# A two-layer diffusion backbone on one core: layer 0's queries and keys in pairs of token tiles, one modulation vector more on VectorE, idle matmuls and paired squares at the start, and layer 1's scores cut 256 + 384

## The chip, the core and the metric

The kernel runs on one core of a Trainium2 chip. The core has TensorE (PE; its weight loads are listed apart as PEld), VectorE (DVE), ScalarE (ACT), GpSimd (POOL) and SyncE (SP), which issues nearly all transfers. The metric is the device time of one execution in microseconds; lower is better.

## The reference

All numbers are float32. 512 latent tokens and 256 context tokens of width 1024 pass two layers; the output is the latent stream.

```python
for i in range(2):
    mod = silu(c) @ ada_w[i] + ada_b[i]          # six vectors of 1024: shift, scale, gate, twice
    u = rms_norm(h, g_mix[i]) * (1 + sc1) + sh1  # latent and context tokens, each with their own c
    if i == 0:   # 2-D neighbourhood attention, 16 heads of 64, relative position bias
        q, k, v = split(u @ na_wqkv); q, k = rms_norm(q, q_gain), rms_norm(k, k_gain)   # per head
        y = softmax(q k^T / 8 + bias over neighbours, and all context keys) v
    else:        # sliding window of 128, 4 key heads, sink logits, rotary
        y = softmax(q k^T / 8 over keys within 128 of the query, all context keys, a sink) v
    h = h + ga1 * (y @ wo)
    h = h + ga2 * (relu((rms_norm(h, g_mlp[i]) * (1 + sc2) + sh2) @ w1) ** 2 @ w2)
```

## The kernel before

**Products.** A float32 product is made of three matmuls of 32-bit "r" operands (fp32r): high times high, high times low, low times high. So each value that enters a matmul is first split by ACT (the high part, a CAST) and DVE or POOL (the rest, a TENSOR_TENSOR). Tokens stand in six tiles of 128: 0 to 3 latent, 4 and 5 context; the model width is eight blocks of 128, called f as features and k as a contraction.

**Start.** `load` (L701) chains the first loads in a fixed order on SP: the latent tokens (`xT`, four loads of two blocks), then, by `LOADS` (L560), eight pairs of loads of `ada01` (the weights of the first two modulation vectors), four loads of `wqkv00` ("w") and the context tokens ("c"). `stats` (L1423) squares each block of the latent tokens and sums over the width with a float32 matmul by `ones` into bank pq4; ACT then takes Ln and Exp (`st.finish`). `ada01(f)` (L1396) multiplies silu(c) by one block's weights, 16 narrow matmuls into pq0 or pq1; `mods01(f)` (L1409) copies that on ACT, turns it with a matmul by `pair`, and DVE makes shift and 1 + scale of it. `mod0` (L1435) makes u of block f, and the products of k = f for the tiles follow in banks pq2 to pq7.

**Layer 0's queries and keys.** Heads go in eight pairs p. `qkv0(p)` (L1010) multiplies six tiles; per tile, `front(t)` copies 128 queries and 128 keys out of PSUM into a ring `xr` (values go to V), `head_norm` (L964) takes four sums of squares and an inverse root by a chain of eight small operations on ACT and DVE, and `dup_mult` and a second multiply write the scaled rows to a ring `natr`. `back(t, nat)` turns them with three PE transposes and splits the result into the operands T1, T2 (queries) and KK (keys): ACT writes the high part, DVE the rest. `attn0(p)` (L1123) makes scores in banks pq0 and pq1, adds the bias read from DRAM tables (`bias_i`, `bias_e`, written at the start by `bias_tables`, L931, as 32 DRAM-to-DRAM copies), and goes on to the softmax, PE transposes and the product with V.

**Modulation.** The vectors 2 to 5 of layer 0 are made beside the attention: `ada_pe` (L767) on PE for the vectors in `PEK` (four groups of eight 32 x 256 matmuls per vector, into pq5; weights `in_ada_w`, two buffers), `ada_rows` (L745) on DVE for those in `DVK` (eight rows per vector, each one load of 512 KB of `in_ada0` into one buffer and three multiply-and-reduce operations: 1024 wide for latents, twice 512 for the context). `DVN[p]` says how many rows are written into stage p.

**Layer 1's scores.** `Head1.front` (L2021) makes per head and latent tile a row of scores: 512 columns for the outer tiles, and for the inner ones (1 and 2) 640, as 512 in pq0 or pq1 and 128 in pq2; DVE shifts and reduces each part.

**What sets the order.** All calls are recorded as steps, and `Plan.search` (L465) lays them out on the engines with its own list of costs and a seeded random search, stretch by stretch; it may also choose between ACT, DVE and POOL for a step that has two forms. So a change in one place moves instructions in all of the program. Every instruction has L548 or a line near it as its line, since all are issued there; tiles tell them apart.

Of the kernel before, what the change touches and what calls it, by code (L numbers as in the profile page):

```python
# [565 lines left out]
def _build(nc, tc, a, es):  # L566
# [443 lines left out]
    def qkv0(p):  # L1010

        T1, T2, KK = views0(p)[:3]

        def products(ps, t, ks):
            sH, sL = tok((uH_lat, uH_ctx), t), tok((uL_lat, uL_ctx), t)
            for k in ks:
                mm(ps, sH(k), W0[p, k][0], k == 0, False)
                mm(ps, sH(k), W0[p, k][1], False, False)
                mm(ps, sL(k), W0[p, k][0], False, k == KT - 1)

        def front(t):
# [12 lines left out]
            gv.tensor_tensor(out=nat[:, 256:384].rearrange("p (h d) -> p h d", h=2), in0=x[:, 128:256].rearrange("p (h d) -> p h d", h=2), in1=r[:, 2:4].unsqueeze(2).broadcast_to([128, 2, DH]), op=ALU.mult)  # L1034
            return nat

        def back(t, nat):
# [3 lines left out]
            pq = pt[:, 0:256].rearrange("p (h n) -> p h n", h=2)
            pk = pt[:, 256:384]
            if t < 3:
                parts = [(0, 128, 64 + t * 128)]
            elif t == 3:
                parts = [(0, 64, 448), (64, 128, 0)]
            else:
                parts = [(0, 128, t * 128)]
# [13 lines left out]
        nats = {}  # L1062
        if p == 0:
            lat, ctx = range(4), range(4, 6)
            for ts, ks in (*((lat, (k,)) for k in range(LATE + 1)), (ctx, range(LATE + 1)), *((range(6), (k,)) for k in range(LATE + 1, KT - LAST))):
# [4 lines left out]
            load0(1, (0, 1))  # L1070

        order = (0, 3, 4, 5, 1, 2) if p == 0 else range(6)
        for j, t in enumerate(order):
            if p == 0:
                products(banks[2 + t], t, range(KT - LAST, KT))
            nats[t] = front(t)
            if p == 0 and j == 1:
                load0(1, (2, 3))
            if 0 < p < 7 and t == 2:
                load0(p + 1, (0, 1))  # L1080
            if 0 < p < 7 and t == 5:
                load0(p + 1, (2, 3))
# [929 lines left out]
    class Head1:  # L2012
# [8 lines left out]
        def front(self):  # L2021
# [2 lines left out]
            nms, sms, ess = small(4), sums_of(h // 2)[:, h % 2 * 4 : h % 2 * 4 + 4], small(4)  # L2024
            for t in (1, 0, 2, 3):
                q0 = t * 128
                ps = p_sc.next()
                inner = t in (1, 2)
                if t == 0:
                    scores(ps, T1, T2, q0, with_context(K, 0))  # L2030
                    mk = FA[:, 4096:4864].rearrange("p (s n) -> p s n", s=2)[:, :, 0:256]
                    col[t] = {0: 256, 1: 384, 4: 0, 5: 128}
                else:
                    scores(ps, T1, T2, q0, with_context(K, t - 1))
                    mk = in2(mask[:, 0:512])
                    col[t] = {t - 1: 256, t: 384, t + 1: 512, 4: 0, 5: 128}
                n0 = nsink[:, h : h + 1]
                if inner:
                    px = banks[2][:, 128 * (t - 1) : 128 * t]
# [1 line left out]
                    n1 = small()
                    v.tensor_tensor_reduce(out=P[t][:, 512:640], in0=px, in1=mask[:, 512:640], scale=-1.0, scalar=n0, op0=ALU.add, op1=ALU.min, accum_out=n1)
                    n0 = n1
                nm = nms[:, t : t + 1]
                v.tensor_tensor_reduce(out=in2(P[t][:, 0:512]), in0=in2(ps), in1=mk, scale=-1.0, scalar=n0, op0=ALU.add, op1=ALU.min, accum_out=nm)
# [190 lines left out]
```

## Time and profile before

| | us |
|---|---|
| median of 3 runs (lowest, highest) | 1545.16 (1543.29, 1547.68) |
| the profiled execution: its time, its span | 1545.8, 1544.0 |
| busy: PE, PEld | 1520.9, 1349.8 |
| busy: DVE, ACT, POOL | 1237.5, 848.2, 228.3 |

The span is what the profiler saw of that execution; 1.8 us lie around it. Busy time is that in which at least one instruction of the engine ran. [...] PE is busy for 99% of the span, and the chain that ended last is 93% PE.

### The profile page before, as it was taken

Reading aid. Unit: us, or ns where it says so; the run is one execution under the profiler, and the core shown is the slowest. Engines: PE = TensorE matmul, PEld = TensorE weight load, DVE = VectorE, ACT = ScalarE, POOL = GpSimd, SP = SyncE. Lnnn points to the kernel's source line nnn. Section 1 sums busy time; section 2 is a strip of 40 time slices with the busy share of each in tenths; the row PEclk is TensorE's granted clock in tenths of the full one; section 3 lists DMA queues with packets and bytes.
Section 4 is the critical chain, followed back from the end, with each engine's and each line's share of the span. In section 5 each row is a group of like instructions: output and inputs, shape, how many; then the busy total and the mean of one; then the engine's idle time right before and its main releaser. Section 6 shows DMA issues by size and latency. Waiting matters only on the chain.

```text
span 1544.0 us, 26106 instructions
## 1 busy us (share of the span) xinstructions
PE 1520.9 (99%) x9541; PEld 1349.8 (87%) x9541; DVE 1237.5 (80%) x2672; ACT 848.2 (55%) x1989; POOL 228.3 (15%) x223
## 2 busy tenths in 40 slices
PE   7999999999999999999999999999999999999999
PEld 4879888898899999999999998888778989898897
DVE  4888888868579998988888778898876897777764
ACT  4676656677366443334433454577784754455551
POOL 1110000101111222200210001321100312111110
PEclk9999999999999999999999999999999999999999
DMA  9554443215435433345444332011145343323321
GB/s 360 156 179 125 137 164 108 75 38 158 148 104 162 129 120 121 125 144 150 155 133 149 97 100 98 21 34 47 34 155 173 105 128 104 101 84 108 97 69 69
DMA packets 81473, 183.88 MB, mean 119 GB/s; under 512 B 9104, under 2 KB 26048, under 8 KB 81344
## 3 DMA queue, kind: packets, MB, share of 16 engines
q1 hardware_dynamic: 81344, 182.21, 37.3%
q8 instruction: 75, 1.23, 0.3%
q14 instruction: 54, 0.44, 0.1%
HBM read 172.64 MB, written 12.68 MB: 120 GB/s over the span
## 4 chain that ended last, share of the span: by engine, by line
PE 93%; DVE 3%; ACT 2%; DMA 1%; issue 1%; SPq 0%; POOL 0%; DVEq 0%; ACTq 0%; POOLq 0%
PE pq L548 93%; DVE FA L548 1%; DVE RA L548 1%; ACT FA L548 1%; DVE R L548 0%; ACT RA L548 0%; DMA R<-inv_d 0%; DMA FA<-bias_e 0%; ACT R L548 0%; DVE smalls L548 0%; DMA FA<-in_xT_dram 0%; SPq L548 0%; ACT smalls L548 0%; DVE mods L548 0%; POOL FA L548 0%
## 5 line engine op out<-in xcount | busy, mean ns | idle before, releaser
L548 PE MATMUL pq<-RA 128*128 128x256 f32 (+2 forms) x5906 | 1067.9, 334 | 8.1 <-DVE RA L548 4.4
L548 PEld LDWEIGHTS pq<-RA 128*128 128x128 f32 x5906 | 919.0, 189 | 94.7 <-issue 6.2
L548 PE MATMUL pq<-RA,R 128*128 128x256 f32 (+2 forms) x1896 | 339.5, 331 | 1.4 <-DVE FA L548 1.4
L548 ACT CAST RA<-FA 128x512 fp32r<-128x512 f32 (+4 forms) x390 | 232.3, 618 | 170.3 <-PE pq L548 124.3
L548 PEld LDWEIGHTS pq<-RA,R 128*128 128x128 f32 x1896 | 299.1, 189 | 26.5 <-DVE FA L548 2.5
L548 DVE TENSOR_TENSOR RA<-FA,RA 128x512 fp32r<-128x512 f32 (+4 forms) x350 | 256.3, 752 | 35.3 <-ACT RA L548 31.5
L548 DVE SCALAR_TENSOR_TENSOR FA<-pq,mods,FA 128x512 f32<-128x512 f32 (+1 forms) x323 | 197.5, 627 | 98.4 <-PE pq L548 96.0
L548 ACT ACTIVATE FA<-FA 128x256 f32<-128x256 f32 (+2 forms) x216 | 102.8, 483 | 58.6 <-DVE FA L548 47.2
L548 ACT CAST R<-FA 128x512 fp32r<-128x512 f32 x107 | 65.2, 619 | 104.3 <-PE pq L548 94.0
L548 PE MATMUL pq<-ident,FA 128*128 128x128 f32 x772 | 118.4, 274 | 2.0 <-issue 1.4
L548 POOL TENSOR_TENSOR RA<-FA,RA 128x512 fp32r<-128x512 f32 (+3 forms) x40 | 57.8, 1450 | 382.4 <-ACT RA L548 330.8
L548 ACT ACTIVATE FA<-FA,smalls 128x512 f32<-128x512 f32 (+1 forms) x120 | 88.7, 740 | 33.6 <-DVE smalls L548 32.8
L548 PEld LDWEIGHTS pq<-ident,FA 128*128 128x128 f32 x772 | 91.8, 141 | 14.0 <-issue 4.6
L548 DVE TENSOR_TENSOR FA<-FA 128x512 f32<-128x512 f32 (+3 forms) x163 | 88.8, 558 | 7.8 <-ACT FA L548 3.8
L548 ACT COPY R<-pq 128x512 f32<-128x512 f32 (+4 forms) x166 | 74.0, 469 | 34.2 <-PE pq L548 33.2
L548 ACT COPY FA<-pq 128x256 f32<-128x256 f32 (+5 forms) x114 | 44.3, 388 | 85.5 <-PE pq L548 82.8
L548 POOL TENSOR_TENSOR FA<-FA,smalls 128x256 f32<-128x256 f32 (+2 forms) x55 | 37.5, 682 | 294.6 <-DVE smalls L548 232.6
L548 DVE CUSTOM_DVE_ANT_0 R<-R,cst 128x512 bf16<-128x512 f32 (+1 forms) x64 | 79.7, 1245 | 0.4 <-DMA R<-in_ada_dram 0.2
L548 ACT CAST RA<-R 128x256 fp32r<-128x256 f32 (+2 forms) x107 | 51.4, 489 | 51.5 <-PE pq L548 46.8
L548 DVE TENSOR_TENSOR R<-FA,R 128x512 fp32r<-128x512 f32 (+1 forms) x101 | 74.3, 743 | 6.5 <-ACT R L548 5.5
L548 POOL TENSOR_TENSOR FA<-FA 128x256 f32<-128x256 f32 (+2 forms) x50 | 46.0, 927 | 186.3 <-ACT FA L548 85.7
L548 PE MATMUL pq<-R 128*64 128x256 f32 (+3 forms) x432 | 67.2, 450 | 1.1 <-DVE FA L548 1.1
(107 smaller groups left out, 1155.3 us busy)
## 6 DMA issues: line engine op xcount, KB each, us to landing
FA<-in_w_dram SPq DMA_DIRECT2D x128, 256.0 KB
FA<-in_w_dram SPq DMA_DIRECT2D x64, 512.0 KB
R<-in_ada_dram SPq DMA_DIRECT2D x54, 512.0 KB
FA<-in_ada_dram SPq DMA_DIRECT2D x26, 512.0 KB
FA<-in_wqkv_dram SPq DMA_DIRECT2D x24, 384.0 KB
FA<-in_ada_w_dram SPq DMA_DIRECT2D x16, 512.0 KB
FA<-in_wo_dram SPq DMA_DIRECT2D x16, 512.0 KB
FA<-in_wq_dram SPq DMA_DIRECT2D x8, 512.0 KB
```

The costliest lines, as they stand in the source:

```text
L548: tc.keep_in_program_order(getattr(e, f)(*map(real, args), **{k: real(x) for k, x in kw.items()}))
```

## The change

There are five edits.

1. `back`, `front` and the new `scaled` treat two tiles at a time: one `head_norm` of eight sums in place of two of four, and one set of wider splits. `xr` becomes one buffer of 512 in place of two of 256, `natr` two of 768 in place of three of 512. The pairs are (0, 3), (4, 5), (1, 2) for p = 0, else (0, 1), (2, 3), (4, 5).
2. Vector 3 of layer 0 goes from `ada_pe` to `ada_rows`: PE has four groups in place of eight, DVE 24 rows in place of 16. `run(ad)` then stands before stage 2, and from there on `p_mm` has two banks (before, from stage 4).
3. In `stats`, DVE adds the squares of two blocks, and PE has four matmuls by `ones` in place of eight.
4. `busy(10, ones)` issues ten 128 x 128 float32 matmuls of `ones` by `ones` into pq7, which nothing reads, ahead of the statistics.
5. An inner tile of layer 1 has its scores as 256 columns (context) in pq2 and 384 (window) in pq0 or pq1: for 16 heads, two tiles and T1 and T2, 64 matmuls of each width.

```diff
-PEK, DVK, DVN = (2, 3), (4, 5), (0, 4, 3, 3, 3, 3)
+PEK, DVK, DVN = (2,), (3, 4, 5), (0, 5, 5, 5, 5, 4)
-    smalls = pool.tile([128, 24, 4], F32, name="smalls", tag="smalls")
+    smalls = pool.tile([128, 24, 8], F32, name="smalls", tag="smalls")
-    xr = Ring(FA, FX + 1536, 256, 2)
+    xr = Ring(FA, FX + 1536, 512, 1)
-    natr = Ring(FA, FX + 7168, 512, 3)
+    natr = Ring(FA, FX + 7168, 768, 2)
...
-        def front(t):
+        def front(t, x, e):
...
-            x = xr.next()
-            sv.copy(x, ps[:, 0:256])
+            sv.copy(x.rearrange("p (w n) -> p w n", w=2)[:, :, 128 * e : 128 * e + 128], ps[:, 0:256].rearrange("p (w n) -> p w n", w=2))
...
+        def scaled(x):
             nat = natr.next()
-            r = head_norm(x, nat[:, 0:256], 4)
-            dup_mult(nat[:, 0:256], x[:, 0:128], r[:, 0:2], 2)
-            gv.tensor_tensor(out=nat[:, 256:384]..., in0=x[:, 128:256]..., in1=r[:, 2:4]..., op=ALU.mult)
+            r = head_norm(x, nat[:, 0:512], 8)
+            dup_mult(nat[:, 0:512], x[:, 0:256], r[:, 0:4], 4)
+            gv.tensor_tensor(out=nat[:, 512:768]..., in0=x[:, 256:512]..., in1=r[:, 4:8]..., op=ALU.mult)
             return nat
-        def back(t, nat):
-            pt = (p_tr if p else p_ad).next()
-            for i in range(3):
-                pe.transpose(pt[:, i * 128 : i * 128 + 128], nat[:, i * 128 : i * 128 + 128], ident[:])
+        def back(ts, nat):
+            pt, pk = [(p_tr if p else p_ad).next() for _ in range(2)]
+            for e in range(2):
+                for h in range(2):
+                    pe.transpose(pt[:, h * 256 + e * 128 :][:, 0:128], nat[:, (2 * e + h) * 128 :][:, 0:128], ident[:])
+            for e in range(2):
+                pe.transpose(pk[:, e * 128 : e * 128 + 128], nat[:, 512 + e * 128 : 640 + e * 128], ident[:])
...
-        order = (0, 3, 4, 5, 1, 2) if p == 0 else range(6)
-        for j, t in enumerate(order):
...
+        last = None
+        for j, ts in enumerate(((0, 3), (4, 5), (1, 2)) if p == 0 else ((0, 1), (2, 3), (4, 5))):
+            x = xr.next()
+            for e, t in enumerate(ts):
...
+                front(t, x, e)
...
+                if not e:
+                    yield
+                    if last:
+                        back(*last)
+            last = ts, scaled(x)
             yield
...
             q = sq.next()
             squared(q, h(f))
-            pe.matmul(ps[:, 0 : st.n], ones[:], q, start=f == 0, stop=f == KT - 1)
+            if f % 2:
+                v.tensor_tensor(out=q, in0=last, in1=q, op=ALU.add)
+                pe.matmul(ps[:, 0 : st.n], ones[:], q, start=f == 1, stop=f == KT - 1)
+            last = q
...
+    def busy(n, x):
+        for _ in range(n):
+            pe.matmul(banks[7][:, 0:128], ones[:], x[:, 0:128], start=True, stop=True)
+
     more(5)
+    busy(10, ones)
...
-        if p < 4:
-            n = (1, 3, 3, 3)[p]
+        if p < 2:
+            n = (1, 4)[p]
...
-                if inner:
-                    px = banks[2][:, 128 * (t - 1) : 128 * t]
-                    scores(px, T1, T2, q0, K[:, q0 + 384 : q0 + 512])
...
+                if t in (1, 2):
+                    px, ps, n1 = banks[2][:, 256 * (t - 1) : 256 * t], ps[:, 0:384], small()
+                    scores(px, T1, T2, q0, K[:, 0:256])
+                    scores(ps, T1, T2, q0, K[:, q0 + 128 : q0 + 512])
+                    col[t] = {t - 1: 256, t: 384, t + 1: 512, 4: 0, 5: 128}
+                    shifted(P[t][:, 0:256], px, mask[:, 0:256], n0, n1)
+                    shifted(P[t][:, 256:640], ps, mask[:, 256:640], n1, nm)
```

The planner lays everything out anew. Three places follow; R00_132 and R00_134 are the buffer of squares, FA_64 and RA_63 the large working buffers, s32_82 silu(c), pair_93 the small turning matrix, and pq0_66 to pq7_73 the PSUM banks.

PE at the very start, before:

```order
L548 MATMUL pq4_70<-R00_132,ones_76 128x512 x8
L548 MATMUL pq0_66<-FA_64,s32_82 32x128 x16
L548 MATMUL pq1_67<-FA_64,s32_82 32x128 x8
L548 MATMUL pq0_66<-pair_93,FA_64 128x4
L548 MATMUL pq1_67<-FA_64,s32_82 32x128 x8
L548 MATMUL pq0_66<-FA_64,s32_82 32x128 x8
L548 MATMUL pq2_68<-RA_63 128x512 x3
L548 MATMUL pq3_69<-RA_63 128x512 x3
L548 MATMUL pq4_70<-RA_63 128x512 x3
L548 MATMUL pq5_71<-RA_63 128x512 x3
L548 MATMUL pq1_67<-pair_93,FA_64 128x4
L548 MATMUL pq0_66<-R00_132,s32_82 32x128 x8
```

and after:

```order
L548 MATMUL pq7_73<-ones_76 128x128 x10
L548 MATMUL pq4_70<-R00_134,ones_76 128x512 x3
L548 MATMUL pq0_66<-FA_64,s32_82 32x128 x8
L548 MATMUL pq4_70<-R00_134,ones_76 128x512
L548 MATMUL pq0_66<-FA_64,s32_82 32x128 x8
L548 MATMUL pq0_66<-pair_93,FA_64 128x4
L548 MATMUL pq1_67<-FA_64,s32_82 32x128 x8
L548 MATMUL pq3_69<-RA_63 128x512 x2
L548 MATMUL pq1_67<-FA_64,s32_82 32x128 x8
L548 MATMUL pq3_69<-RA_63 128x512
L548 MATMUL pq1_67<-pair_93,FA_64 128x4
L548 MATMUL pq2_68<-RA_63 128x512 x3
```

The idle matmuls are first; `ada01(0)` moved in among the statistics, and `ada01(1)` with its `pair` matmul moved in among the first three products (pq3) of k = 0, where it stood behind all twelve.

ACT at the start, before (squares of the statistics in R00_132, Ln, Exp, the split of `wqkv00`'s first load, the copy of `ada01(0)`, the first high part of u):

```order
L548 ACTIVATE sg_83<-cst_79 128x16
L548 ACTIVATE R00_132<-FA_64 128x512 x4
L548 ACTIVATE FA_64<-pq4_70,eps_77 128x512
L548 ACTIVATE FA_64<-FA_64 128x512
L548 CAST RA_63<-FA_64 128x1024
L548 COPY FA_64<-pq0_66 128x128
L548 ACTIVATE RA_63<-FA_64,mods0_84 128x512
L548 COPY FA_64<-pq1_67 128x128
```

and after:

```order
L548 ACTIVATE R00_134<-FA_64 128x512
L548 ACTIVATE sg_83<-cst_79 128x16
L548 ACTIVATE R00_134<-FA_64 128x512 x3
L548 ACTIVATE FA_64<-pq4_70,eps_77 128x512
L548 COPY FA_64<-pq0_66 128x128
L548 ACTIVATE FA_64<-FA_64 128x512
L548 CAST RA_63<-FA_64 128x1024
L548 ACTIVATE RA_63<-FA_64,mods0_84 128x512
```

The copy of pq0 now stands ahead of Exp and of the split, which it stood behind.

SP from the end of the bias tables to the first reads of them (`in_wqkv02` are weights of p = 2, `in_ada_w` the weights for `ada_pe`, `in_ada0` a row for DVE), before:

```order
L548 DMA bias_i_88<-in_rpb_i_dram 16x8x256
L548 DMA bias_e_89<-in_rpb_dram 16x8x128
L548 DMA FA_64<-in_wqkv02_dram 128x768 x2
L548 DMA FA_64<-in_ada_w_dram 128x1024 x2
L548 DMA FA_64<-in_ada0_dram 128x1024
L548 DMA FA_64<-bias_i_88 128x256 x2
L548 DMA FA_64<-bias_e_89 64x128 x4
L548 DMA FA_64<-in_wqkv02_dram 128x768 x2
```

and after:

```order
L548 DMA bias_i_88<-in_rpb_i_dram 16x8x256
L548 DMA bias_e_89<-in_rpb_dram 16x8x128
L548 DMA FA_64<-in_wqkv02_dram 128x768 x2
L548 DMA FA_64<-in_ada0_dram 128x1024
L548 DMA FA_64<-bias_i_88 128x256
L548 DMA FA_64<-bias_e_89 64x128 x2
L548 DMA FA_64<-bias_i_88 128x256
L548 DMA FA_64<-bias_e_89 64x128 x2
```

The `in_ada_w` loads moved ahead, to places among the earlier table copies, so that three loads of weights stand between the tables' last copy and their first read, where there were five; and the reads for the first head now come before those for the second.

More of the change, by code (lines that the diff above doesn't have):

```diff
@@ L1033, in front @@
-            dup_mult(nat[:, 0:256], x[:, 0:128], r[:, 0:2], 2)
-            gv.tensor_tensor(out=nat[:, 256:384].rearrange("p (h d) -> p h d", h=2), in0=x[:, 128:256].rearrange("p (h d) -> p h d", h=2), in1=r[:, 2:4].unsqueeze(2).broadcast_to([128, 2, DH]), op=ALU.mult)
-            return nat
-        def back(t, nat):
-            pt = (p_tr if p else p_ad).next()
-            for i in range(3):
-                pe.transpose(pt[:, i * 128 : i * 128 + 128], nat[:, i * 128 : i * 128 + 128], ident[:])
[L1041 to L1048, printed above, removed]
+            r = head_norm(x, nat[:, 0:512], 8)
@@ new lines, in scaled, with place @@
+            dup_mult(nat[:, 0:512], x[:, 0:256], r[:, 0:4], 4)
+            gv.tensor_tensor(out=nat[:, 512:768].rearrange("p (h d) -> p h d", h=4), in0=x[:, 256:512].rearrange("p (h d) -> p h d", h=4), in1=r[:, 4:8].unsqueeze(2).broadcast_to([128, 4, DH]), op=ALU.mult)
+            return nat
+        def back(ts, nat):
[5 more added lines that the diff above has]
+                pe.transpose(pk[:, e * 128 : e * 128 + 128], nat[:, 512 + e * 128 : 640 + e * 128], ident[:])
+            pq, pk = pt.rearrange("p (h n) -> p h n", h=2), pk[:, 0:256].rearrange("p (e n) -> p e n", e=2)
+            def place(t):
+                return ([(0, 64, 448), (64, 128, 0)] if t == 3 else [(0, 128, t * 128 + (64 if t < 3 else 0))])
+            parts = []
+            for e, t in enumerate(ts):
+                for lo, hi, at in place(t):
+                    lo, hi = lo + 128 * e, hi + 128 * e
+                    if parts and parts[-1][1] == lo and parts[-1][2] + lo - parts[-1][0] == at:
+                        parts[-1] = (parts[-1][0], hi, parts[-1][2])
+                    else:
+                        parts.append((lo, hi, at))
@@ L1052, in back @@
                 ops.append((T1[:, :, at : at + hi - lo], T2[:, :, at : at + hi - lo], pq[:, :, lo:hi], gq, gq))
-            at = (t + 2) % 6 * 128
+            a0, a1 = ((t + 2) % 6 for t in ts)
             for i in range(2):
-                ops.append((KK[0:64, i, at : at + 128], KK[64:128, i, at : at + 128], pk[64 * i : 64 * i + 64], gk[64 * i : 64 * i + 64], gk[0:64]))
+                K = KK[:, i].rearrange("p (b n) -> p b n", n=128)[:, a0 : a1 + 1 : a1 - a0]
+                ops.append((K[0:64], K[64:128], pk[64 * i : 64 * i + 64], gk[64 * i : 64 * i + 64], gk[0:64]))
             for oH, oL, of, by, by_l in ops:
@@ L1060, in back @@
                 v.scalar_tensor_tensor(out=oL, in0=of, scalar=by_l, in1=oH.bitcast(F32), op0=ALU.mult, op1=ALU.subtract)
-        nats = {}
         if p == 0:
@@ L1070, in qkv0 @@
             load0(1, (0, 1))
-        order = (0, 3, 4, 5, 1, 2) if p == 0 else range(6)
-        for j, t in enumerate(order):
[L1074 to L1082, printed above, removed]
+        last = None
+        for j, ts in enumerate(((0, 3), (4, 5), (1, 2)) if p == 0 else ((0, 1), (2, 3), (4, 5))):
+            x = xr.next()
+            for e, t in enumerate(ts):
+                if p == 0:
+                    products(banks[2 + t], t, range(KT - LAST, KT))
+                front(t, x, e)
+                if p == 0 and 2 * j + e == 1:
+                    load0(1, (2, 3))
+                if 0 < p < 7 and t == 2:
+                    load0(p + 1, (0, 1))
+                if 0 < p < 7 and t == 5:
+                    load0(p + 1, (2, 3))
+                if not e:
[3 more added lines that the diff above has]
+            last = ts, scaled(x)
             yield
-            if j:
-                back(order[j - 1], nats[order[j - 1]])
-        back(order[5], nats[order[5]])
+        back(*last)
         yield
@@ L2026, in front, with shifted @@
                 q0 = t * 128
-                ps = p_sc.next()
-                inner = t in (1, 2)
-                if t == 0:
+                ps, nm, n0 = p_sc.next(), nms[:, t : t + 1], nsink[:, h : h + 1]
+                def shifted(out, ps, mk, n0, nm):
+                    v.tensor_tensor_reduce(out=out, in0=ps, in1=mk, scale=-1.0, scalar=n0, op0=ALU.add, op1=ALU.min, accum_out=nm)
+                if t in (1, 2):
[5 more added lines that the diff above has]
+                    shifted(P[t][:, 256:640], ps, mask[:, 256:640], n1, nm)
+                elif t == 0:
                     scores(ps, T1, T2, q0, with_context(K, 0))
-                    mk = FA[:, 4096:4864].rearrange("p (s n) -> p s n", s=2)[:, :, 0:256]
                     col[t] = {0: 256, 1: 384, 4: 0, 5: 128}
+                    shifted(in2(P[t][:, 0:512]), in2(ps), FA[:, 4096:4864].rearrange("p (s n) -> p s n", s=2)[:, :, 0:256], n0, nm)
                 else:
                     scores(ps, T1, T2, q0, with_context(K, t - 1))
-                    mk = in2(mask[:, 0:512])
                     col[t] = {t - 1: 256, t: 384, t + 1: 512, 4: 0, 5: 128}
-                n0 = nsink[:, h : h + 1]
-                if inner:
-                    px = banks[2][:, 128 * (t - 1) : 128 * t]
-                    scores(px, T1, T2, q0, K[:, q0 + 384 : q0 + 512])
[L2041 to L2045, printed above, removed]
+                    shifted(in2(P[t][:, 0:512]), in2(ps), in2(mask[:, 0:512]), n0, nm)
                 s.activation(P[t], P[t], AF.Exp, bias=nm, scale=-1.0, accum_out=sms[:, t : t + 1])
```

## The prediction

> **What bounds the kernel now.** I read the page first (PE busy 99%, chain 93% PE), then the busy time by stretch, then PE's waits, then the chain from the start on. By stretch (from:to and length in us; busy PE, PEld, DVE, ACT and POOL, with instructions; granted clock, DMA share, GB/s):
>
> ```profile
> 5.58:15.41 9.83, 9.82 (x16) 4.00 (x16) 2.09 (x4) 1.89 (x3) 0.00 (x0) 1.00 1.02 383
> 15.41:20.92 5.51, 3.33 (x83) 2.27 (x82) 2.23 (x5) 3.18 (x6) 0.00 (x0) 1.00 1.06 385
> 20.92:37.88 16.96, 15.75 (x159) 12.05 (x159) 9.39 (x19) 8.48 (x20) 4.39 (x4) 0.90 1.00 396
> 37.88:68.75 30.87, 30.62 (x202) 25.42 (x203) 24.71 (x68) 16.95 (x44) 2.86 (x9) 1.00 0.52 127
> 68.75:82.99 14.24, 11.18 (x90) 8.98 (x89) 12.70 (x41) 11.02 (x36) 1.80 (x3) 1.00 0.85 256
> 80.00:100.00 20.00, 17.81 (x135) 15.70 (x131) 17.41 (x56) 16.27 (x46) 2.45 (x4) 0.91 0.41 127
> 82.99:300.00 217.01, 213.59 (x1445) 188.89 (x1446) 188.58 (x544) 146.75 (x427) 22.55 (x33) 0.99 0.42 134
> ...
> 983.00:1162.00 179.00, 177.54 (x1226) 146.54 (x1226) 152.37 (x462) 132.51 (x327) 30.42 (x39) 1.00 0.20 63
> ```
>
> After 83 us PE hardly waits (3.4 us of 217, 1.5 of 179): there only less work on PE shortens the kernel. The first 83 us are another matter: PE idles 2.2 + 1.2 + 0.3 + 3.1 us, runs the statistics slowly, and waits in a chain. From the chain, in order of time:
>
> ```profile
> 1.19 3.69 DMA FA<-in_xT_dram
> ...
> 5.58 9.91 PE pq L548 x16
> ...
> 16.77 1.04 ACT RA L548
> ...
> 27.83 7.53 PE pq L548 x60
> ...
> 75.84 6.13 DMA FA<-bias_e
> ```
>
> PE is held by the statistics to 15.4, then by ACT (the weights' split at 16.77 ahead of the small copy) to 20.92, and at 82 by the bias table's read. But DMA is saturated to 37.88 (share 1.0): what lands by then can't land sooner, only be used sooner.
>
> **The start, step by step.** Rows of the timeline (start, length, engine, instruction):
>
> ```profile
> 10.02 0.34 PEld L548 LDWEIGHTS pq<-R,ones 128*128 128x128 f32 x1 [0.52 <-issue]
> 10.87 0.34 PEld L548 LDWEIGHTS pq<-R,ones 128*128 128x128 f32 x1 [0.52 <-issue]
> 11.44 0.63 ACT L548 ACTIVATE R<-FA 128x512 f32<-128x512 f32 x1 [1.56 <-DMA FA<-in_xT_dram]
> 12.09 0.69 DVE L548 TENSOR_TENSOR R<-FA 128x512 f32<-128x512 f32 x1 [1.99 <-PE pq L548]
> 12.32 0.19 PEld L548 LDWEIGHTS pq<-R,ones 128*128 128x128 f32 x1 [0.24 <-issue]
> 12.75 0.19 PEld L548 LDWEIGHTS pq<-R,ones 128*128 128x128 f32 x1 [0.24 <-issue]
> 15.52 0.69 ACT L548 ACTIVATE FA<-pq,eps 128x512 f32<-128x512 f32 x1 [3.45 <-PE pq L548]
> 16.24 0.63 ACT L548 ACTIVATE FA<-FA 128x512 f32<-128x512 f32 x1
> 17.71 0.26 ACT L548 COPY FA<-pq 128x128 f32<-128x128 f32 x1
> 20.15 0.72 ACT L548 ACTIVATE RA<-FA,mods 128x512 fp32r<-128x512 f32 x1 [2.18 <-DVE FA L548]
> 25.56 0.28 PE L548 MATMUL pq<-pair,FA 128*128 128x4 f32 x2
> 37.88 12.73 PE L548 MATMUL pq<-RA 128*128 128x512 f32 x54 [0.18 <-ACT RA L548]
> ```
>
> Eight float32 matmuls of 512 are 16 passes; a pass takes 0.86 us at first (10.02 to 10.87) and 0.43 later. Ten idle ones of 128 are 20 passes of a quarter, 20 x 0.215 = 4.3 us from about 1.1 us on, while PE has nothing; their cover is the wait for the first tokens (4.9), and without it they would cost at most those 4.3 less 3.8. Pairing needs one DVE addition (0.69) per two blocks; with the last tokens at 11.44, square 0.65, addition 0.69 and handoffs bring the last pair to about 12.9, and `ada01(0)`'s first half stands ahead. Then two passes: the statistics end at 13.9 to 15.6 (warm to cold) instead of 15.41; I take 14.3, as the passes from 11.4 on were fast even here.
>
> Then Ln 0.69 + copy 0.26 + Exp 0.63 + split 1.04 (beside DVE's product) + high part 0.72 + 0.15 of handoffs = 3.5 us, where it was 5.51, as the chain of `ada01(0)` and the split no longer stand in a row. First product at 17.8 instead of 20.92: 3.1 us less. Next, block 1's `pair` matmul stood behind twelve products of k = 0 (25.56), and k = 1 began at 27.83; now it stands after three. PE's rows up to the context's first products hold 48 products where they held 36. One product takes (12.73 - 0.40) / 53 = 0.233 us, so twelve are 2.8 us. The last of these blocks lands late whatever PE does, so I put the context's start at 35.3 rather than 37.88 (2.6 less). With one `ada01` more left to do behind it (about 0.9) the gain at 68.75 is 2.8 + 2.6 - 0.9 = 4.5 us. Its ends: 0, if the landings hold the block behind, and 7.
>
> **From 68.75 to 82.99** PE idles 3.06 us, and its first `ada_pe` group there takes 2.0 us instead of 1.0:
>
> ```profile
> 78.98 1.12 PE L548 MATMUL pq<-FA,s 128*32 128x256 f32 x16
> 79.46 0.16 PEld L548 LDWEIGHTS pq<-FA,s 128*32 128x32 f32 x8 [0.32 <-DMA FA<-in_ada_w_dram]
> 97.98 1.07 PE L548 MATMUL pq<-FA,s 128*32 128x256 f32 x16
> ```
>
> Its weights now come among the table copies, so sooner. SP's table copies start when the fourth split of weights frees a buffer, so they follow PE's and ACT's lead forward, and three loads instead of five stand ahead of the first bias read, which took 6.13 us to land. I take 1.5 of the 3.06 and 0.9 of that group: 2.4 us; ends 0 and 4. The late queries and keys wait next: three wide chains instead of six narrow ones, but each longer. The clock 0.91 over 80 to 100 us (20 x 0.09 = 1.8 us lost) follows that idling; I count half of it back, 0.8. The start in all: 4.5 + 2.4 + 0.8 = 7.7 us.
>
> [...]
>
> **Vector 3 off PE.** Groups of 16 records take 1.07 us (97.98, with what runs on into the next), about 1.1 with the change of shape; four groups and two transposes of 0.11 go: 4 x 1.1 + 0.2 = 4.6 us of PE work, in a stage that PE bounds. Ends 3.6 and 5. In its place DVE gets eight rows:
>
> ```profile
> L548 DVE CUSTOM_DVE_ANT_0 FA<-FA,RA,cst 128x1024 f32<-128x1024 f32 x16 | 22.1, 1382 | 0.2
> L548 DVE CUSTOM_DVE_ANT_0 FA<-FA,RA,mods 128x512 bf16<-128x512 f32 x16 | 12.0, 747 | 0.2
> L548 DVE TENSOR_REDUCE smalls<-FA 128x4 f32<-128x256 f32 x70 | 28.9, 414 | 7.3 <-ACT FA L548 6.2 <-issue 0.3
> L548 DVE TENSOR_REDUCE smalls<-pq 128x2 f32<-128x512 f32 x16 | 11.0, 685 | 1.5 <-PE pq L548 1.3
> L548 DVE SCALAR_TENSOR_TENSOR smalls<-smalls 128x4 f32<-128x4 f32 x140 | 24.2, 173 | 2.1
> L548 DVE SCALAR_TENSOR_TENSOR RA<-pq,cst,RA 64x128 fp32r<-64x128 f32 x96 | 33.4, 349 | 2.5 <-ACT RA L548 0.4
> L548 DVE SCALAR_TENSOR_TENSOR RA<-pq,cst,RA 128x256 fp32r<-128x256 f32 x40 | 19.2, 480 | 7.8 <-ACT RA L548 7.5
> ```
>
> Eight rows are 8 x (1.38 + 2 x 0.75 + 3 x 0.08) = 25 us. **Pairs** give DVE back: 24 chains less of four small operations (24 x 4 x 0.173 = 16.6), 48 sums of 0.414 become 24 of about 0.685 (3.4), 96 key splits of 0.349 become 48 of 0.48 (10.5): 30 us. So DVE's load in the stage stays at 188.6 of 217 or falls a little, ACT's falls, and PE's work is the same: 0 for the end, as PE covers it (between 3 lost, as `xr` is one buffer and PE's next pair may wait for it, and 3 won).
>
> **Layer 1's scores.** By runs of equal matmuls, 512 columns take 0.233 us, and
>
> ```profile
> 344.78 5.70 PE L548 MATMUL pq<-RA 128*128 128x384 f32 x30
> 1002.67 5.04 PE L548 MATMUL pq<-RA 128*128 128x256 f32 x40
> 86.31 0.93 PE L548 MATMUL pq<-ident,FA 128*128 128x128 f32 x7
> ```
>
> 384 take (5.70 - 0.34) / 29 = 0.185 at most, 256 (5.04 - 0.28) / 39 = 0.122. For 128 the trace has no run; transposes of 128 take (0.93 - 0.27) / 6 = 0.11, a quarter of 512 would be 0.058. 512 + 128 against 384 + 256 is 0.343 against 0.307 (a gain of 2.3 us in 64) or, by the quarter, 0.291 (a loss of 1). Transposes too load 128 x 128 weights for 128 columns, so I take theirs and 2.6 (384 without the gaps in its run). DVE's two parts add up as before: 0.
>
> **Sum.** 7.7 + 4.6 + 2.6 = 14.9 us off the profiled execution's 1545.8, which is 0.6 above the median: 1530.3 for the median, say 1530. A second layout of the whole program may move a wait of 1 to 2 us elsewhere; I give it 0.
>
> **Rivals.** (A) The start's gain does not last: the bias read, or the landings of the first 37 us, hold PE to the old times. For it speaks the DMA share of 1.0; against it that 36 of 144 products were done when it ended. Then only 4.6 + 2.6 are left: 1538.
>
> (B) Slower: DVE waits for its rows. They have one buffer, and SP's two closest loads of rows are
>
> ```profile
> 252.22 0.33 SPq L548 DMA_DIRECT2D FA<-in_ada_dram x1
> 260.94 0.33 SPq L548 DMA_DIRECT2D FA<-in_ada_dram x1
> ```
>
> 8.7 us apart. 24 rows are then at least 209 us; they have about 105 to 325, 9.2 each. From 9.2 on, each us more is 24 us on DVE; the stage's 28 us of idle DVE cover the first 1.2, and at 11.0 (24 x 1.8 less 28) 15 us reach PE, which eats the gain; at 11.4, 10 more: 1555. Against it: DVE waited 0.2 us before these operations in all 16 rows.
>
> (C) Nothing to measure: pairs hold two of the three banks for transposes and the single `xr`, and PE waits as much in stages 1 to 6 as the rest gains (some 2.5 us per stage): 1545. Against it speaks ACT's and DVE's smaller load, and the second bank for products from stage 2 on.
>
> **Chances.** Forecast (1523 to 1534.5) 0.63; A (to 1540) 0.22; C 0.08; B 0.07. The range 1523 to 1540 holds the first two. 0.3% (4.6 us) is about what a measurement here tells from no change: faster 0.85, same 0.08, slower 0.07.
>
> **What would show it.** After: fast passes from the first statistics on; first product near 17.8; k = 1 near 22; the first softmax near 75; four `ada_pe` groups in all; DVE without waits for `in_ada`; layer 1's attention 2 to 3 us shorter. I am wrong if the first softmax stays at 82, or if PE's waits between it and the MLP grow beyond 5 us.

## The result, and the profile after

The changed kernel takes 1529.84 us (median; 1529.64 to 1531.21) against 1544.22 of the kernel before on the same chip: a ratio of 0.9907, 95% interval 0.9895 to 0.9919, 14.4 us less. The forecast was 1530, range 1523 to 1540. The time and the direction were right; of the sum's three terms one held, as the runs below show.

The changed kernel by stretches (columns as in the first fence of the prediction), and then PE's timeline at the places named there:

```profile
5.58:15.20 9.62, 7.11 (x41) 2.31 (x40) 5.89 (x17) 2.85 (x7) 0.00 (x0) 0.82 1.00 372
15.20:17.98 2.78, 1.03 (x19) 0.68 (x19) 1.89 (x4) 2.44 (x5) 0.00 (x0) 1.00 1.02 417
17.98:37.88 19.90, 18.67 (x168) 13.92 (x168) 12.73 (x25) 9.68 (x21) 3.01 (x3) 0.91 1.03 401
37.88:62.46 24.58, 23.78 (x194) 19.12 (x189) 17.22 (x41) 11.27 (x27) 2.33 (x7) 1.00 0.60 161
62.46:80.67 18.21, 16.66 (x140) 14.56 (x140) 13.93 (x37) 11.43 (x31) 2.47 (x2) 1.00 0.85 244
83.00:300.00 217.00, 215.66 (x1427) 196.27 (x1426) 185.22 (x436) 133.57 (x341) 19.02 (x18) 1.00 0.39 119
```

```profile
1.06 4.63 PE L548 MATMUL pq<-ones 128*128 128x128 f32 x20 [1.06 <-DVE ones L548]
9.26 3.48 PE L548 MATMUL pq<-R,ones 128*128 128x512 f32 x4 [1.28 <-DVE R L548]
17.98 0.89 PE L548 MATMUL pq<-RA 128*128 128x512 f32 x2 [1.33 <-ACT RA L548]
30.32 0.38 PE L548 MATMUL pq<-pair,R 128*128 128x4 f32 x2 [1.23 <-ACT R L548]
80.67 1.34 PE L548 MATMUL pq<-RA 128*128 128x512 f32 x4 [1.55 <-DVE smalls L548]
```

The first product is at 17.98 (17.8 was forecast), but the first scores are at 80.67, not near 75. From 83 to 300 us PE idles 1.3 us, where it idled 3.4 before, with 3 us less on DVE. So much less was won at the start than forecast, and more later.

To see where, I compare times at equal progress. For each trace I add up the matmuls of products, scores and transposes, in the order of their starts and from the span's start, at usual intervals (0.227, 0.173, 0.119 and 0.11 us for 512, 384, 256 and 128 columns, where the medians from start to start of neighbours of equal width are 0.228, 0.174, 0.120 and 0.109 us in the trace of the kernel before; those with V I count at half), and leave out statistics, idle matmuls and the first two modulation vectors. A record lasts longer than the interval, 0.40, 0.34, 0.29 and 0.27 us on average, so records overlap and busy time alone does not give PE's rate. The columns 69 to 960 say how far each kernel is from the kernel before, in us, where it has done as much as that had at this time. The orders make the `ada_pe` groups at different times, so up to 174 a group counts as 1.07 us of work; from 313 on it does not, so that the four groups that edit 2 saves are a gain. In the column 1200, behind layer 1's attention, as much is left to do, so that the smaller work of edit 5 is a gain. Negative is ahead. The last column is the ratio of the runs less 1, times 1544.

| kernel | 69 | 100 | 127 | 174 | 313 | 464 | 960 | 1200 | by the runs |
|---|---|---|---|---|---|---|---|---|---|
| changed | -0.5 | -4.4 | -4.5 | -6.0 | -12.4 | -11.7 | -12.1 | -16.3 | -14.4 |
| only edits 3, 4 | -1.6 | -4.8 | -3.1 | -2.2 | -2.9 | -3.0 | -3.1 | -4.1 | 0.0 |
| only edit 2 | +1.4 | -1.5 | -1.3 | 0.0 | -7.1 | -6.7 | -6.3 | -6.5 | -2.9 |
| only edit 1 | +1.9 | -1.2 | +0.8 | +0.8 | -1.2 | +0.2 | +1.1 | +0.6 | +4.9 |
| only edit 5 | +0.1 | -1.7 | -1.8 | -1.8 | -1.9 | -1.2 | -1.0 | -4.3 | -1.2 |
| before, other seed | +0.5 | -3.2 | -3.0 | -3.5 | -6.1 | -6.6 | -6.6 | -6.4 | -3.4 |
| changed, other seed | -2.2 | -5.2 | -5.3 | -6.3 | -13.5 | -12.4 | -11.2 | -13.9 | -10.2 |
| changed less edit 1 | -3.7 | -4.6 | -2.7 | -2.5 | -10.0 | -10.3 | -11.7 | -14.5 | -12.2 |
| changed less edits 3, 4 | +0.5 | -2.4 | -1.6 | -3.1 | -9.8 | -9.5 | -9.0 | -11.2 | -6.5 |
| before, vector 3 not issued | -1.2 | -3.1 | -3.2 | -3.1 | -3.8 | -3.2 | -2.7 | -3.5 | -1.2 |

The row of edit 5 and the last row keep the order of the kernel before up to 464 us (the last one throughout), and yet stand 1.7 and 3.1 us ahead at 100. That is scatter between executions of one order, at the place where the bias table is read and the first scores wait. Set against those two, the changed kernel is ahead at 127 us by 1.3 to 2.7 us; of its lead, 7.9 us come between 127 and 313 us, in the stages of layer 0's attention (4.3 of them are the four groups that are not made), and 4.2 between 960 and 1200, in layer 1's. All rows end 1.9 to 4.7 us further ahead here than by the runs: the profiled execution of the kernel before took 1545.8 us, 1.6 above the median of its runs, and the others lose 0.3 to 3.3 us against it behind 1200 us.

### The profile page after: what moved, and what is told of

It is laid out like the page before. It is cut to its first block, busy times and chain, and to the rows that moved or that the text cites. A ratio compares the mean times of both kernels' runs of the same rounds, so it can differ in the third digit from the quotient of the medians.

```text
span 1528.0 us, 25568 instructions
## 1 busy us (share of the span) xinstructions
PE 1513.9 (99%) x9487; PEld 1348.9 (88%) x9487; DVE 1229.2 (80%) x2510; ACT 820.2 (54%) x1845; POOL 208.4 (14%) x196
## 4 chain that ended last, share of the span: by engine, by line
PE 94%; DVE 3%; DMA 1%; SPq 1%; ACT 0%; issue 0%; POOL 0%; DVEq 0%
PE pq L548 94%; DVE FA L548 1%; SPq L548 1%; DVE RA L548 1%; DMA bias_e<-in_rpb_dram 0%; DMA FA<-in_xT_dram 0%; DVE smalls L548 0%; DMA FA<-bias_e 0%; ACT FA L548 0%; ACT RA L548 0%; DVE R L548 0%; POOL FA L548 0%; DVE amod L548 0%; DVE mods L548 0%; ACT R L548 0%
## 5 line engine op out<-in xcount | busy, mean ns | idle before, releaser
L548 PE MATMUL pq<-RA 128*128 128x256 f32 (+2 forms) x5906 | 1085.9, 334 | 4.9 <-DVE smalls L548 2.7
L548 PEld LDWEIGHTS pq<-RA 128*128 128x128 f32 x5906 | 920.4, 189 | 89.5 <-DVE smalls L548 6.5
L548 PE MATMUL pq<-RA,R 128*128 128x256 f32 (+2 forms) x1896 | 355.6, 332 | 0.0
L548 ACT CAST RA<-FA 128x512 fp32r<-128x512 f32 (+4 forms) x390 | 232.0, 618 | 185.9 <-PE pq L548 149.2
L548 PEld LDWEIGHTS pq<-RA,R 128*128 128x128 f32 x1896 | 301.1, 188 | 23.9 <-DVE FA L548 0.3
L548 DVE TENSOR_TENSOR RA<-FA,RA 128x512 fp32r<-128x512 f32 (+4 forms) x351 | 261.0, 760 | 40.3 <-ACT RA L548 36.5
L548 DVE SCALAR_TENSOR_TENSOR FA<-pq,mods,FA 128x512 f32<-128x512 f32 (+1 forms) x323 | 196.4, 626 | 84.9 <-PE pq L548 83.1
L548 ACT ACTIVATE FA<-FA 128x384 f32<-128x384 f32 (+2 forms) x198 | 101.2, 518 | 66.9 <-DVE FA L548 59.6
L548 PE MATMUL pq<-ident,FA 128*128 128x128 f32 x770 | 124.5, 274 | 0.6 <-DVE FA L548 0.5
L548 ACT CAST R<-FA 128x512 fp32r<-128x512 f32 x107 | 65.2, 618 | 95.6 <-PE pq L548 85.8
L548 ACT ACTIVATE FA<-FA,smalls 128x512 f32<-128x512 f32 (+1 forms) x120 | 88.9, 742 | 48.3 <-DVE smalls L548 48.0
L548 PEld LDWEIGHTS pq<-ident,FA 128*128 128x128 f32 x770 | 92.8, 141 | 13.8 <-issue 2.8
L548 POOL TENSOR_TENSOR RA<-FA,RA 128x384 fp32r<-128x384 f32 (+3 forms) x39 | 56.8, 1461 | 353.3 <-ACT RA L548 240.3
L548 ACT COPY R<-pq 128x512 f32<-128x512 f32 (+4 forms) x172 | 76.4, 466 | 47.7 <-PE pq L548 44.3
L548 DVE TENSOR_TENSOR FA<-FA 128x512 f32<-128x512 f32 (+3 forms) x149 | 84.1, 577 | 6.1 <-ACT FA L548 5.5
L548 DVE TENSOR_TENSOR R<-FA,R 128x512 fp32r<-128x512 f32 (+1 forms) x105 | 77.6, 745 | 8.3 <-ACT R L548 6.4
L548 ACT COPY FA<-pq 128x256 f32<-128x256 f32 (+4 forms) x111 | 42.6, 388 | 75.0 <-PE pq L548 63.2
L548 ACT CAST RA<-R 128x256 fp32r<-128x256 f32 (+2 forms) x107 | 50.5, 489 | 54.0 <-PE pq L548 47.7
L548 DVE CUSTOM_DVE_ANT_0 R<-R,cst 128x512 bf16<-128x512 f32 (+1 forms) x64 | 75.5, 1180 | 0.9 <-DMA R<-in_ada_dram 0.9
L548 POOL TENSOR_TENSOR FA<-FA 128x256 f32<-128x256 f32 (+2 forms) x58 | 49.0, 855 | 196.5 <-ACT FA L548 91.5
L548 PE MATMUL pq<-R 128*64 128x256 f32 (+3 forms) x432 | 67.2, 450 | 0.0
L548 POOL TENSOR_TENSOR FA<-FA,smalls 128x256 f32<-128x256 f32 (+1 forms) x28 | 29.1, 1044 | 243.9 <-DVE smalls L548 194.0
```

Source lines behind the costliest of these rows:

```text
L548: tc.keep_in_program_order(getattr(e, f)(*map(real, args), **{k: real(x) for k, x in kw.items()}))
```

## The experiments

### Each edit alone

Four kernels are the kernel before with one group of edits each, as in the diff of the change: edits 3 and 4 (`stats` and `busy`), edit 2 (`PEK`, `DVK`, `DVN` and `if p < 2`), edit 1 (`front`, `scaled`, `back` and the rings), edit 5 (`Head1.front`).

Edits 3 and 4:

```diff
-            pe.matmul(ps[:, 0 : st.n], ones[:], q, start=f == 0, stop=f == KT - 1)
+            if f % 2:
+                v.tensor_tensor(out=q, in0=last, in1=q, op=ALU.add)
+                pe.matmul(ps[:, 0 : st.n], ones[:], q, start=f == 1, stop=f == KT - 1)
+            last = q
...
+    busy(10, ones)
```

> The kernel before with edits 3 and 4 alone (four statistics matmuls by `ones` instead of eight, ten idle matmuls first). By the ledger of the two traces (at the first product with V the same products have been made, 2.98 us sooner and with one `ada_pe` group of 1.1 us more behind them): -4.1 us, 1540.1. By the prediction's step: -7.7 us, 1536.5. By rival A (the bias read or the landings hold the rest, the start's gain does not last): less than 1.5 us, 1543 or more.

Measured: 1544.47 us, ratio 1.0000 (0.9991 to 1.0009). Its lead in the table, 4.8 us at 100 us, is 3.1 at 127 and 2.9 at 313, where the two other executions of the order of the kernel before have 1.8 to 3.2 and 1.9 to 3.8: against those, nothing of it is left.

Edit 2:

```diff
-PEK, DVK, DVN = (2, 3), (4, 5), (0, 4, 3, 3, 3, 3)
+PEK, DVK, DVN = (2,), (3, 4, 5), (0, 5, 5, 5, 5, 4)
```

> The kernel before with edit 2 alone (vector 3 by eight more rows on DVE, four `ada_pe` groups less). If PE bounds the stages and DVE has room without the pairs too: -4.6 to -5.2 us, 1539 to 1539.6. If edit 2 needs the DVE time that the pairs set free (DVE would have 188.6 + 25 of 217 us in stages 0 to 4): PE waits for DVE there and the gain shrinks below 2 us, 1542 or more.

Measured: 1541.15 us, ratio 0.9981 (0.9972 to 0.9989), a gain of 2.9 us, between the two expectations.

Edit 1:

> The kernel before with edit 1 alone (queries and keys by pairs of tiles). By the prediction: 0, within 1.5 us of 1544.2, as PE's work is the same. Rival: the pairs carry what the ledger finds beside the priced terms (layer 0's attention has 1.7 us less of PE waits and fewer waits than forecast): -2 to -4 us, 1540 to 1542. By rival C (single `xr`, two banks for transposes): slower by 2 us or more.

Measured: 1549.32 us, ratio 1.0032 (1.0020 to 1.0044): 4.9 us slower, the way of rival C. The place is not rival C's, though: in the table it is 0.8 us behind at 127 and 1.2 ahead at 313, and in the trace it loses 3.3 us behind 1200 us, where the code is the same.

Edit 5:

> The kernel before with edit 5 alone (inner tiles of layer 1 as 256 + 384). By the matmul counts of the two traces at one price per width: -1.7 us, 1542.5. By the prediction's term: -2.6 us, 1541.6. If PE's waits in layer 1's attention also fall by the 1.9 us found between the traces because of this edit: -3.6 us, 1540.6. If that was another layout of the program: between -1 and -2.6.

Measured: 1542.76 us, ratio 0.9992 (0.9983 to 1.0001), 1.2 us, and the interval just holds no change. At equal progress the place of the edit, 960 to 1200 us, gives 3.3. The order of PE is that of the kernel before until 730 us.

Alone, the edits sum to +0.8 us; together they give -14.4. Either they help each other, or something else moves with them.

### Another order of the same work

Every kernel is laid out anew by a seeded search. Two kernels change only its seed, and two take one edit out of the changed kernel.

```diff
-        rnd, pe = random.Random(1), self.ALL.index("PE")
+        rnd, pe = random.Random(2), self.ALL.index("PE")
```

The kernel before:

> The kernel before, with only the seed of the layout search changed (1 to 2); the same instructions in another order. Theory L (the four edits alone gave 0, -2.7, +5.5 and -1.0 us, which do not add to -14.3, because each change draws another layout and layouts differ by several us): 2 to 6 us away from 1543.8, either way. Theory I (the edits help each other, layouts of the same work are alike): within 1.5 us of 1543.8.

Measured: 1540.63 us, ratio 0.9978 (0.9968 to 0.9988): 3.4 us faster with the same work.

The changed kernel:

> The changed kernel with only the seed of the layout search changed (1 to 2). Theory L: 2 to 6 us away from 1529.8, and rather slower (1532 to 1536), if the layout drawn first was a good one. Theory I: within 1.5 us of 1529.8.

Measured: 1533.57 us, ratio to before 0.9934 (0.9922 to 0.9947): 3.7 us slower than the changed kernel by the medians. Theory L holds: the order alone moves either kernel by some 3.5 us. With seed 1 the change gives 14.4 us, with seed 2 it gives 1540.63 - 1533.57 = 7.1, on average 10.7. Here is the stretch from 83 to 300 us by the windows (columns as above), first in the kernel before:

```profile
83.00:300.00 217.00, 213.58 (x1445) 188.88 (x1446) 188.57 (x544) 146.74 (x427) 22.55 (x33) 0.99 0.42 134
```

then in its order from the second seed:

```profile
83.00:300.00 217.00, 216.50 (x1472) 191.72 (x1471) 183.50 (x539) 152.11 (x440) 29.36 (x38) 1.00 0.42 132
```

and with edit 1 alone:

```profile
83.00:300.00 217.00, 212.41 (x1422) 188.17 (x1421) 174.81 (x412) 132.20 (x333) 23.86 (x18) 1.00 0.40 127
```

With the second seed PE idles 0.5 us in place of 3.4 and gets 27 matmuls more done. With pairs alone DVE is busy 14 us less and ACT 15, and PE still idles 4.6: the load of DVE and ACT alone doesn't decide there.

Edit 1 taken out of the changed kernel:

> The changed kernel without edit 1 (queries and keys by single tiles again), all else as changed. Theory I: the start's lead was lost between 85 and 150 us where edits 3 and 4 stood alone (5.9 us ahead at 80 us, 1.9 behind at 150), as chains on ACT and DVE for single tiles hold PE there; so without pairs 8 to 12 us of the 14.3 go: 1538 to 1542. If the pairs are worth nothing (the prediction's 0): 1529 to 1532. Theory L: anything between, 1530 to 1540, with no place of its own for the loss.

Measured: 1532.14 us, ratio to before 0.9921 (0.9907 to 0.9934), 2.3 us slower than the changed kernel by the medians. Theory I's loss of 8 to 12 us did not come; 2.3 is less than a seed moves. That the pairs save the whole lead of the start is refuted; in the table this kernel loses 1.9 us of its lead between 100 and 127 us, where the changed kernel keeps its own, so 2 us may be theirs.

Edits 3 and 4 taken out:

> The changed kernel without edits 3 and 4 (eight statistics matmuls, no idle matmuls). By the ledger of before and after (4.1 us at the first product with V): 1534. By the prediction's 7.7: 1537.5. If the start's gain does not last (alone it gave 0): 1530.

Measured: 1537.86 us, ratio 0.9958 (0.9944 to 0.9971), 8.0 us slower by the medians. This is as large as the prediction's term, but its place is another: at 100 us it stands 2.0 us behind the changed kernel, at 313 us 2.6, at 960 us 3.1 and at 1200 us 5.1. More than half of it is lost behind 313 us, where the code is the same.

### The same order, with one thing taken away

To be free of the search, four kernels keep the planned order word for word and change only what is issued: a step may carry a list `emit` that is issued in place of its calls.

```diff
-            for f, args, kw in step.calls:
+            for f, args, kw in step.calls if step.emit is None else step.emit:
```

The idle matmuls of edit 4:

```diff
-            pe.matmul(banks[7][:, 0:128], ones[:], x[:, 0:128], start=True, stop=True)
+            pe.matmul(banks[7][:, 0:128], ones[:], x[:, 0:128], start=True, stop=True).emit = []
```

> The changed kernel in its own order, with the ten idle matmuls planned but not issued. In the changed kernel the clock was full from 6.4 to 9.8 us, half from 9.8 to 13.2 and from 20.0 to 23.4: two of the four statistics pairs ran at half speed in spite of the idle matmuls. Theory: they buy nothing that lasts, within 1 us of 1529.8. The prediction's step (statistics end 13.9 warm, 15.6 cold): 1.3 us later, 1531.1, if the first product follows the statistics.

Measured: 1530.27 us, ratio to before 0.9900 (0.9886 to 0.9913); the changed kernel has 0.9907. They buy nothing that the runs show.

More idle matmuls (`idle(n)` is n matmuls of `ones` by `ones` into pq7, 128 columns each; `plan.idle` holds three, issued ahead of the first product):

```diff
-                pe.matmul(ps[:, 0 : st.n], ones[:], q, start=f == 1, stop=f == KT - 1)
+                x = pe.matmul(ps[:, 0 : st.n], ones[:], q, start=f == 1, stop=f == KT - 1)
+                x.emit = x.calls + idle((0, 3, 0, 1, 0, 2, 0, 0)[f])
...
+            if plan.idle and step.eng == "PE" and step.calls[0][1][1].dtype == R32:
+                step.emit, plan.idle = plan.idle + step.calls, []
```

> The changed kernel in its own order with nine idle matmuls more, in the gaps of PE between the statistics pairs (3, 1, 2) and before the first product (3). [...] If the landings (DMA share 1.0 to 38 us) set the time of what follows: the first product sooner, the end within 0.7 us of 1529.8.

Measured: 1529.21 us, ratio 0.9892 (0.9876 to 0.9908), 0.6 us below the changed kernel by the medians, with intervals that overlap; it is not shown to be faster. The first product came sooner, and this gave nothing at the end. PE's timeline without idle matmuls:

```profile
9.24 3.78 PE L548 MATMUL pq<-R,ones 128*128 128x512 f32 x4 [0.74 <-DVE R L548]
...
18.66 0.88 PE L548 MATMUL pq<-RA 128*128 128x512 f32 x2 [1.50 <-ACT RA L548]
...
29.71 0.39 PE L548 MATMUL pq<-pair,R 128*128 128x4 f32 x2 [1.23 <-ACT R L548]
```

and with nine more (two lines were put in ahead, so L548 is L550 here):

```profile
17.31 0.87 PE L550 MATMUL pq<-RA 128*128 128x512 f32 x2
...
26.01 0.64 PE L550 MATMUL pq<-R,s 128*32 128x128 f32 x16 [0.23 <-DMA R<-in_ada_dram]
26.58 0.39 PE L550 MATMUL pq<-pair,R 128*128 128x4 f32 x2
27.24 0.64 PE L550 MATMUL pq<-R,s 128*32 128x128 f32 x16 [0.28 <-DMA R<-in_ada_dram]
28.78 0.39 PE L550 MATMUL pq<-pair,R 128*128 128x4 f32 x2 [0.89 <-ACT R L550]
```

The first product comes at 18.66, 17.98 or 17.31 us with none, ten or nineteen idle matmuls, and in the third kernel PE then waits for the loads of `in_ada` at 26 and 27 us. PE's order is the same in the three, so the same matmul can be compared: at 38 us the kernel without idle matmuls is 0.6 us ahead of the changed kernel, and that with nineteen is level with it. The first scores come at 79.89, 80.67 and 80.46. So the kernel that made its first product last is then in front; the clock, in the last section, fits this.

Vector 3 in the order of the kernel before:

```diff
-            with together():
+            with together() as x3:
+                if kind == 3 and layer == 0:
+                    x3.emit = []
```

> The kernel before in its own order, with the 64 narrow matmuls of vector 3's four `ada_pe` groups planned but not issued (vector 3 is left out; its loads, its copy and its two transposes stay). If PE bounds those stages, as the prediction's second term says: -4.3 to -4.8 us from 1544, 1539.2 to 1539.7. If PE's waits for DVE and ACT in these stages set the time: less than 2 us.

Measured: 1543.27 us, ratio 0.9992 (0.9982 to 1.0002): 1.2 us, with an interval from 2.8 to none, where 4.3 to 4.8 were expected. Vector 3's four groups stood between 178 and 231 us. By the windows, the two stages around them (from one product with V to the second after it) in the kernel before:

```profile
155.06:247.90 92.84, 92.15 (x621) 81.35 (x620) 80.94 (x233) 58.38 (x172) 7.80 (x12) 1.00 0.45 144
```

and in this one:

```profile
151.96:244.07 92.11, 89.15 (x558) 79.45 (x557) 80.84 (x233) 58.52 (x172) 7.80 (x12) 1.00 0.45 146
```

What PE waited for in them (us, times, longest), before:

```profile
PE pq L548 <- DVE RA L548: 0.5, 1, 0.5
PE pq L548 <- DVE smalls L548: 0.2, 1, 0.2
```

and without the groups:

```profile
PE pq L548 <- ACT FA L548: 0.8, 1, 0.8
PE pq L548 <- DVE RA L548: 0.7, 1, 0.7
PE pq L548 <- DVE smalls L548: 0.7, 2, 0.6
PE pq L548 <- DVE R L548: 0.3, 1, 0.3
PE pq L548 <- ACT R L548: 0.3, 1, 0.3
```

The four groups are gone (63 records less, as the second window takes in one more at its end), PE is busy 3.0 us less, and the two stages are 0.73 us shorter. The waits for ACT and DVE rise from 0.7 to 2.8 us: in this order the groups stood where PE would have waited. Behind them its lead in the table shrinks again, from 3.8 us at 313 to 2.7 at 960.

The rows on DVE that replace them, in the order of the changed kernel:

```diff
+            if layer == 0 and kind == 3:
+                y.emit = [("tensor_tensor_reduce", (), kw(lo + 64, out[:, 0:64]))]
```

> The changed kernel in its own order, with the 24 operations of vector 3's eight rows 64 columns wide in place of 512 and 1024 (most of vector 3's sums are left out; the loads stay): some 18 us less on DVE. The prediction's cover (DVE has idle time beside PE): within 1 us of 1529.8. By rival B in part (the rows delay what PE waits for): 2 us or more faster, 1527.8 or less.

Measured: 1529.14 us, ratio 0.9894 (0.9880 to 0.9907), 0.7 us below the changed kernel by the medians. Its stages:

```profile
83.00:300.00 217.00, 215.67 (x1426) 196.46 (x1425) 170.27 (x437) 133.35 (x342) 18.74 (x17) 1.00 0.40 122
```

DVE does 15 us less there (170.3 against 185.2) and PE's busy time is the same to 0.01. The work of the eight rows on DVE is hidden, as forecast.

## Why the prediction was right or wrong, point by point

**The total** was right, but partly by luck. The prediction gave "a second layout of the whole program" 0, and a wait of 1 to 2 us. It moves each kernel by about 3.5 us, here both ways in favour of the change: the kernel before had the worse of its two orders, the changed one the better. With both seeds averaged, 10.7 us would be the change's, and with seed 2 on both sides it is 7.1. What the start lacked came back between 127 and 313 us.

**The start (7.7)** is the step that failed. The chain to the first product was right: 17.98 for 17.8, 2.9 us sooner than before. The statistics end at 14.55 us for the 14.3 that I took, though four of their eight passes are slow (3.48 us); fast passes throughout, as I expected of the idle matmuls, did not come. What failed comes behind it. The lead at 68.75, for which I added up 4.5 us, is 0.5 at 69 us; what took it down from 2.9 is not shown. And the first scores, near 75 by the forecast, are held by the bias table, as rival A has it. I let the copies of the table follow PE's lead forward. They do begin sooner, at 43.60 us for 45.04, but SP has four loads of `in_ada_w` among them and issues the last copy 2.4 us later than before. SP in the kernel before:

```profile
69.18 0.60 SPq L548 DMA_DIRECT2D bias_e<-in_rpb_dram  x1
```

in the changed kernel:

```profile
71.62 0.60 SPq L548 DMA_DIRECT2D bias_e<-in_rpb_dram  x1
```

and the chain from this copy by the table's read to the first scores:

```profile
71.62 3.87 DMA bias_e<-in_rpb_dram
75.50 4.25 DMA FA<-bias_e
80.67 4.33 PE pq L548 x29
```

That the landings of the first 37 us hold PE, the other half of rival A, is not shown by this. The 2.4 and 0.8 us from 68.75 on also rested on one execution. The timeline of PE has the first scores of the kernel before at

```profile
82.99 2.04 PE L548 MATMUL pq<-RA 128*128 128x512 f32 x4 [1.32 <-DVE smalls L548]
```

and in two other executions of its order (vector 3 not issued, then edit 5 alone) at

```profile
81.11 1.25 PE L548 MATMUL pq<-RA 128*128 128x512 f32 x4 [0.62 <-DVE smalls L548]
```

```profile
82.46 1.26 PE L548 MATMUL pq<-RA 128*128 128x512 f32 x4 [0.62 <-DVE smalls L548]
```

so the changed kernel's 80.67 is 0.4 to 2.3 us sooner, not 8; that is near the prediction's own sign of being wrong, a first softmax that stays at 82. These four matmuls took 2.04 us in the first and 1.25 and 1.26 in the others. The granted clock of the first is 0.91 from 80 to 100 us; that of the others is 1.00 from 68.75 to 82.99 us and in the mean from 83 us (to 120 and to 300), though PE idled 2.4 us from 68.75 to 82.99 there too (3.06 in the first). So the runs don't show that the clock follows the idling, as I took it, and the 0.8 us for the clock was not the change's to win. At 100 us the changed kernel is ahead of these two executions by 1.3 and 2.7 us. Still, at the end the kernel without edits 3 and 4 is 8.0 us slower in the order that it got; since more than half of that arises behind 313 us, and the seed moves 3.5, the runs don't say what share is the edits'.

**Vector 3 (4.6)**: the count was right (four groups, PE work by the same intervals), the claim "in a stage that PE bounds" was not. Taking only the work away gives 0.7 us in its two stages and about 1.2 in all. With a new order, edit 2 alone gives 2.9. Between 127 and 313 us, where the four groups (4.3 us) stood, the five orders with edit 2 gain 5.8 to 8.2 us, 7.5 on average, and the five others 3.1 or less, 1.1 on average. So the work seems to be worth something once the planner packs the stages anew, but PE's busy share of 99% did not show what it is worth: where PE lost the work alone, it waited for ACT and DVE in its place.

**The rows on DVE (0)** were right: thinning them changes nothing, and in the groups of instructions of the changed kernel 0.3 us of idle time stand ahead of each of the three operations of all 24 rows. Rival B didn't happen.

```profile
L548 DVE CUSTOM_DVE_ANT_0 FA<-FA,RA,cst 128x1024 f32<-128x1024 f32 x24 | 30.8, 1284 | 0.3
L548 DVE CUSTOM_DVE_ANT_0 FA<-FA,RA,cst 128x512 bf16<-128x512 f32 x24 | 20.9, 869 | 0.3 <-DMA FA<-in_ada_dram 0.3
L548 DVE CUSTOM_DVE_ANT_0 FA<-FA,RA,mods 128x512 bf16<-128x512 f32 x24 | 17.8, 743 | 0.3
```

**The pairs (0)**: 4.9 us slower alone and 2.3 us faster within the change. Both lie near the spread of orders; 0 was a fair value, with ends of 3 either way that were too near.

**Layer 1's scores (2.6)** came out in size. Between 960 and 1200 us the five orders with edit 5 (the changed kernel, edit 5 alone, the other seed and the two with an edit taken out) gain 4.2, 3.3, 2.7, 2.8 and 2.2 us, 3.1 on average; the five without it gain 1.0, 0.2, 0.5 and 0.8 and lose 0.2, 0.5 on average. The difference is 2.6. That the edit alone gave 1.2 us by the runs, with an interval from 2.6 to none, shows how much the rest of an order can take away.

**What stays open**: how the gain divides among edits 1, 2 and 3 with 4, and what took the first product's lead down by 69 us. Two seeds are too few for a spread, and the changed kernel without edit 2 was not run.

## What to carry to other kernels

Where a planner lays out the whole program for each version, run two or three orders of both versions before a difference of some us is put down to an edit; the order itself moved this one by 3.5. To price one term, keep the order and issue less. A PE that is busy 99% need not bound its stages: taking PE work away where it filled the waits of a chain on ACT and DVE gained little here (0.73 us in two stages for 3.0 us of work) until the order was made anew, and a wait seen in one execution should be seen in a second one before it is a term of a sum. Ask whether the transfers that the next stage waits for come forward with a lead on PE; here the lead at the first product was 2.9 us, the last copy of the table went back by 2.4, and the first scores came 0.4 to 2.3 us sooner.
